# Both FFN products of a decoder layer by one level of Strassen's algorithm

## The chip, the cores and the metric

The kernel runs on one core of a Trainium2 chip. A core has TensorE (PE, with its weight loads as PEld), VectorE (DVE), ScalarE (ACT), GpSimd (POOL) and SyncE (SP, which here only issues transfers). The metric is device time in microseconds of one execution, the median of several runs.

## The reference, cut to what matters

One inference step of a one-layer decoder: 1024 prompt tokens and 8 x 4 sample tokens, together T = 1056 columns of width 1024. The token mixer (two attention branches, gates, output projection) stands first; the change lies behind its gates.

```python
def conv_ffn(h, conv_prev, w_up, conv_w, conv_b, w_down):
    t = h.shape[1]
    a, g = jnp.split(jnp.einsum('ntd,df->ntf', h, w_up), 2, axis=-1)
    ap = jnp.concatenate([conv_prev.astype(a.dtype), a], axis=1)
    c = conv_b
    for j in range(CONV_W):
        c = c + conv_w[j] * ap[:, j:j + t]
    y = jnp.einsum('ntf,fd->ntd', jax.nn.gelu(c, approximate=True) * g, w_down)
    return y, ap[:, t:]
...
    mixed = jax.nn.sigmoid(ga) * y_a + jax.nn.sigmoid(gb) * y_b
    return jnp.einsum('ntd,de->nte', mixed, w_out), new
...
    x = x + rmsnorm(mix, g_mix_post)
    f, new_conv = conv_ffn(rmsnorm(x, g_ffn_pre), conv_prev, w_up, conv_w, conv_b, w_down)
    x = x + rmsnorm(f, g_ffn_post)
```

D_MODEL is 1024, D_FF 4096, CONV_W 3; everything is in float32.

## The kernel before

Activations lie with features on the 128 partitions and tokens along the columns. Each float32 operand of a large product is *cut* in two parts, h and l, of a reduced format (fp32r in the rows), and a product takes three matmuls, wh x xh, wl x xh and wh x xl (`product`, L218; the matmul is L229). A weight unit of 128 x 1024 is loaded by SP into a `raw` tile (two of them), copied by ACT to wh (L94) and subtracted by POOL to wl (L95); the class `Stream` does this a few units ahead.

The tokens go through the output projection in three chunks of CH = 352 columns. For each chunk and each of 8 row tiles there are 24 matmuls; ACT squares the result and writes it to `mixed`. `post` (L1109) is a generator with the two norms that follow (after the mixer, before the FFN) of the chunk before; `advance` moves it on by steps between the products, by a table of numbers. A norm's statistics go through `spread` (L138): matmuls `ss` with ones add the squares over partitions, ACT and DVE make the factor 1/sqrt (`rstd_of`), DVE puts it on diagonals `dg`, and matmuls `rb` spread it to all partitions, in PSUM. The result, h2h and h2l, stays in SBUF for all tokens.

The FFN has 32 feature tiles f. For each, the up product makes a and g (two parts of three chunks, 24 matmuls each); behind part a, DVE runs the three-tap convolution over 1072 columns (L1214 to L1216) and ACT gelu (L1217); behind part g, DVE multiplies to u, ACT and DVE cut u to uh and ul (L1221, L1222). The down product of f (`down`, L1196: 24 groups of three matmuls of 352 columns, each added by DVE into `acc`, L1206) is put in portions of four groups behind the following up products. The last NL = 3 feature tiles' down products come in a last stage by 288, 256, 256 and 256 tokens, with the last norm (`final`, L1305) of each stretch beside the next one's matmuls.

The order on each engine is that in which the code emits instructions; each engine works through its own in order. All loads and stores of weights and activations here are issued by SP.

## Time and profile before

| what | value |
|---|---|
| time, median of 3 runs | 1975.89 us (1975.85 to 1976.13) |
| span of the profiled execution | 1977.6 us |
| PE busy | 1946.5 us (98%), 12418 instructions |
| DVE, ACT, POOL busy | 1015.3, 596.0, 527.1 us |
| output projection (732.60 to 862.80) | PE busy 127.47 of 130.20 us |
| FFN (862.80 to 1912.00) | PE busy 1049.20 of 1049.20 us |
| last stage (1912.00 to 1962.00) | PE busy 47.09 of 50.00 us |
| the FFN's traffic | 55 GB/s on a mean |

The profiled execution's span is 1.7 us longer than the median time. Busy time is the time in which an engine has an instruction under way; matmuls overlap, so their pace is read from the distance of their starts. Where a row of a timeline ends in a bracket, it says how long the engine stood idle before it and what ended that. The granted clock is a share of TensorE's full speed.

### The profile page before, as it was taken

Reading aid. Unit: us, or ns where it says so; the run is one execution under the profiler, and the core shown is the slowest. Engines: PE = TensorE matmul, PEld = TensorE weight load, DVE = VectorE, ACT = ScalarE, POOL = GpSimd, SP = SyncE. Lnnn points to the kernel's source line nnn. Section 1 sums busy time; section 2 is a strip of 40 time slices with the busy share of each in tenths; the row PEclk is TensorE's granted clock in tenths of the full one; section 3 lists DMA queues with packets and bytes.
Section 4 is the critical chain, followed back from the end, with each engine's and each line's share of the span. In section 5 each row is a group of like instructions: output and inputs, shape, how many; then the busy total and the mean of one; then the engine's idle time right before and its main releaser. Section 6 shows DMA issues by size and latency. Waiting matters only on the chain.

```text
span 1977.6 us, 30477 instructions
## 1 busy us (share of the span) xinstructions
PE 1946.5 (98%) x12418; PEld 1872.5 (95%) x12418; DVE 1015.3 (51%) x2221; ACT 596.0 (30%) x1365; POOL 527.1 (27%) x437
## 2 busy tenths in 40 slices
PE   7999999999999999999999999999999999999996
PEld 7977888888999999999999999999999999999996
DVE  7354437878611144774544545554455555445446
ACT  4365654444221134452211121121112112111233
POOL 3200025344333313422222222122222212222224
PEclk8999999999999999999999999999999999999998
DMA  5222145443422244711211121111111111111132
GB/s 204 71 73 75 69 116 168 137 131 122 162 80 94 84 153 180 289 54 65 75 65 54 64 85 50 58 54 43 54 44 43 53 34 54 44 54 44 43 116 88
DMA packets 63532, 175.15 MB, mean 89 GB/s; under 512 B 12720, under 2 KB 31216, under 8 KB 62192
## 3 DMA queue, kind: packets, MB, share of 16 engines
q1 hardware_dynamic: 61728, 172.72, 25.5%
q8 instruction: 97, 1.59, 0.3%
q10 hardware_dynamic: 1664, 0.49, 0.1%
q14 instruction: 43, 0.35, 0.1%
HBM read 160.21 MB, written 57.84 MB: 110 GB/s over the span
## 4 chain that ended last, share of the span: by engine, by line
PE 91%; DVE 5%; issue 1%; ACT 1%; POOL 0%; DMA 0%; SPq 0%; POOLq 0%; DVEq 0%; ACTq 0%
PE dense L229 84%; PE S L411 2%; PE O L483 2%; PE PT L471 2%; DVE sq L202 1%; DVE mixed L1319 1%; PE ss L144 0%; DVE mixed L1320 0%; DVE P L422 0%; PE rb L153 0%; DVE part L630 0%; DVE P L458 0%; DMA x<-in_x 0%; DVE d L434 0%; PE O L488 0%
## 5 line engine op out<-in xcount | busy, mean ns | idle before, releaser
L95 POOL TENSOR_TENSOR wl<-raw,wh 128x1024 fp32r<-128x1024 f32 (+1 forms) x110 | 261.1, 2373 | 996.6 <-ACT wh L94 787.2
L229 PE MATMUL dense<-h2h,wh 128*128 128x352 f32 x1536 | 495.7, 323 | 0.0
L229 PE MATMUL dense<-h2l,wh 128*128 128x352 f32 x1536 | 494.4, 322 | 0.0
L229 PE MATMUL dense<-h2h,wl 128*128 128x352 f32 x1536 | 493.0, 321 | 0.0
L1206 DVE TENSOR_TENSOR mixed<-dense,mixed 128x352 f32<-128x352 f32 x672 | 321.2, 520 | 147.5 <-PE dense L229 147.5
L229 PE MATMUL dense<-hh,wh 128*128 128x352 f32 x960 | 319.9, 336 | 2.4 <-ACT wh L94 1.9
L229 PE MATMUL dense<-hh,wl 128*128 128x352 f32 x960 | 307.5, 324 | 1.5 <-DVE wl L95 1.5
L229 PE MATMUL dense<-hl,wh 128*128 128x352 f32 x960 | 308.2, 325 | 0.0
L229 PEld LDWEIGHTS dense<-h2h,wl 128*128 128x128 f32 x1536 | 289.3, 188 | 0.0
L229 PEld LDWEIGHTS dense<-h2l,wh 128*128 128x128 f32 x1536 | 288.6, 188 | 0.0
L229 PEld LDWEIGHTS dense<-h2h,wh 128*128 128x128 f32 x1536 | 288.2, 188 | 0.0
L229 PE MATMUL dense<-uh,wdh 128*128 128x352 f32 (+2 forms) x792 | 254.8, 322 | 0.0
L229 PE MATMUL dense<-uh,wdl 128*128 128x352 f32 (+2 forms) x792 | 254.1, 321 | 0.0
L229 PE MATMUL dense<-ul,wdh 128*128 128x352 f32 (+2 forms) x792 | 254.0, 321 | 0.0
L229 PEld LDWEIGHTS dense<-hh,wh 128*128 128x128 f32 x960 | 180.9, 189 | 23.1 <-issue 14.0
L229 PEld LDWEIGHTS dense<-hh,wl 128*128 128x128 f32 x960 | 182.0, 190 | 1.9 <-DVE wl L95 1.9
L229 PEld LDWEIGHTS dense<-hl,wh 128*128 128x128 f32 x960 | 182.4, 191 | 0.0
L1239 ACT COPY a<-dense 128x352 f32<-128x352 f32 (+1 forms) x96 | 42.7, 445 | 372.3 <-PE dense L229 372.2
L1255 DVE TENSOR_TENSOR u<-dense,cv 128x352 f32<-128x352 f32 (+1 forms) x96 | 49.1, 511 | 206.1 <-PE dense L229 204.8
L229 PEld LDWEIGHTS dense<-uh,wdl 128*128 128x128 f32 x792 | 151.0, 191 | 0.0
L229 PEld LDWEIGHTS dense<-ul,wdh 128*128 128x128 f32 x792 | 150.8, 190 | 0.0
L229 PEld LDWEIGHTS dense<-uh,wdh 128*128 128x128 f32 x792 | 150.7, 190 | 0.0
(254 smaller groups left out, 2476.9 us busy)
## 6 DMA issues: line engine op xcount, KB each, us to landing
raw<-in_w_up SPq DMA_DIRECT2D x64, 512.0 KB, 3.4
out_s<-in_cache SPq DMA_DIRECT2D x32, 1022.0 KB, 8.0
raw<-in_w_in SPq DMA_DIRECT2D x40, 512.0 KB, 3.6
kv<-in_kv_s SPq DMA_DIRECT2D x64, 256.0 KB, 4.0
raw<-in_w_down SPq DMA_DIRECT2D x32, 512.0 KB, 3.5
out_s<-in_cache SPq DMA_DIRECT2D x8, 1016.0 KB
x<-in_x SPq DMA_DIRECT2D x12, 528.0 KB, 6.4
x2d<-mixed SPq DMA_DIRECT2D x3, 1408.0 KB
```

What stands on the lines that cost most here:

```text
L95: (eng or pool).tensor_tensor(l, raw, as32(h), op=OP.subtract)
L202: eng.tensor_tensor(o, o, x, op=OP.add)
L229: pe.matmul(ps, lhsT=w, rhs=x, start=(i == 0), stop=(i == len(mm) - 1))
L411: pe.matmul(S[h][:, 0:nk], lhsT=q[r, i * 128:(i + 1) * 128], rhs=k[r, blocks[i][0] * 128:blocks[i][0] * 128 + nk], start=True, stop=True)
L471: pe.transpose(PT[:, o:o + 128], s["P"][:, h, j * 128:(j + 1) * 128], ident)
L483: pe.matmul(O[64 * h:64 * h + 64, 0:128], lhsT=vt[:, kb * 128 + 64 * h:kb * 128 + 64 * h + 64], rhs=s["PTs"][:, (h * m + j) * 128:(h * m + ...
L1206: dve.tensor_tensor(acc[:, ct, cs], ps, acc[:, ct, cs], op=OP.add)
L1239: act.copy(at[:, 2 + c * CH:2 + c * CH + n], ps[:, :n])
L1255: dve.tensor_tensor(us_[:, c * CH:c * CH + n], ps[:, :n], cv[:, c * CH:c * CH + n], op=OP.mult)
L1319: (pool if own else dve).tensor_tensor(m, m, rs if own else rb, op=OP.mult)
```

## The change

Strassen's algorithm splits both operands of a product in 2 x 2 blocks and makes the four result blocks from seven products of sums of blocks instead of eight products of blocks; the form used here (Winograd's) has four sums of each operand.

*Output projection.* It runs in NQ = 4 quarters of CQ = 264 tokens instead of three chunks. `post` norms a quarter; for quarters 2 and 3 DVE also makes the token sums T1 to T4 out of the quarters' blocks, and `second_ops` cuts these operands. `advance` moves `post` by other numbers: ss and rb of a norm come in one step.

*Up product.* A unit m is one part (a or g) of a pair of feature tiles. For each of its seven products p, `up` issues two groups of 12 matmuls of 264 columns. POOL makes four sums of weight blocks for each m, and `cut_block` cuts a block of 128 x 512 (ACT copies, POOL subtracts) LA = 4 products ahead. `evac` takes results out of PSUM with DVE adds (ACT copies for p = 0). The convolution of a pair's second tile comes behind product 5 of part a, that of the first behind product 6, gelu behind each; u is made behind products of part g.

*u through DRAM.* `u_sums` makes four sums of u's blocks on DVE, and SP stores seven operands for each pair; the down product loads them back.

*Down product.* It comes after the whole up product: seven products, one at a time, each summed over all 16 pairs in all eight PSUM banks (four row tiles by two column groups; the last product in two halves of tokens). A step is 24 matmuls of 264 columns (12 in the halves) and needs a block of weights and an operand of u, loaded LOAD = 5 and cut CUT = 3 steps ahead; the weight sums are DVE's. `down_evac` adds a product's banks into acc. The last norm's parts (`squares_of`, `final`) are moved on by two steps behind each down step.

Besides, there are four `raw` tiles instead of two, tiles of the attention's phase have another side of the memory, and tables of the convolution have tiles of their own.

```diff
+CQ = 264
+NQ = 4
...
-        raw = wpool.tile([128, n], F32, name="raw", tag="raw", bufs=2, padded_shape=[128, 1024])
+        raw = wpool.tile([128, n], F32, name="raw", tag="raw", bufs=4, padded_shape=[128, 1024])
...
+    def cut_mixed(q, g, eng, new):
...
+        src = mixed[:, 4 * g:4 * g + 4, q * CQ:(q + 1) * CQ]
+        act.copy(h, src)
+        eng.tensor_tensor(l, src, as32(h), op=OP.subtract)
...
+    def op_cut(name, j, src, c=None):
...
+        dve.tensor_tensor(l, src, as32(h), op=OP.subtract)
...
+    def post(q, sums):
...
+        last = q == NQ - 1
+        g = spread(sums, CQ)
         next(g)
         yield
         rb = next(g)
...
         for ct in range(KT):
             m = mixed[:, ct, cs]
             dve.tensor_tensor(m, m, rb, op=OP.mult)
...
+            (dve if last or ct in (1, 3, 5) else pool).tensor_tensor(m, m, x3[q][ct // 4][:, ct % 4], op=OP.add)
+            sq.append(quarter("sq"))
+            act.activation(sq[-1], m, AF.Square)
+            if len(sq) > 2:
+                total(sums, sq.pop(0), pool if last else dve)
             if ct == KT - 1:
...
+        g = spread(sums, CQ)
         next(g)
         yield
         rb = next(g)
...
+        for k in range(KT):
+            o = x3[q][k // 4][:, k % 4] if last else mixed[:, k, cs]
+            dve.scalar_tensor_tensor(o, mixed[:, k, cs], gains[:, 2, k:k + 1], rb, op0=OP.mult, op1=OP.mult)
+            if k % 2:
...
+        t2 = x3[2][c]
+        for j in range(2):
+            b1, b2 = rows(2 * j, q), rows(4 + 2 * j, q)
+            b11, b21 = rows(2 * j, q - 2), rows(4 + 2 * j, q - 2)
+            dve.tensor_tensor(b11, b1, b11, op=OP.subtract)
+            dve.tensor_tensor(t2[:, 2 * j:2 * j + 2], b2, b11, op=OP.subtract)
+            dve.tensor_tensor(b1, b2, b1, op=OP.subtract)
+            dve.tensor_tensor(b21, b21, t2[:, 2 * j:2 * j + 2], op=OP.subtract)
+            yield
...
+    def second_ops():
...
+        for name in ("T2", "T3", "T4", "B22", "T1"):
...
+                    q = 2 + c
+                    src = {"T2": x3[2][c][:, 2 * j:2 * j + 2], "T3": rows(2 * j, q), "T4": rows(4 + 2 * j, c),
+                           "B22": rows(4 + 2 * j, q), "T1": rows(2 * j, c)}[name]
+                    op_cut(name, j, src, c)
+                yield
...
+    PRODUCTS = (("A11", "B11"), ("A12", "B21"), ("S2", "T2"), ("S3", "T3"), ("A22", "T4"), ("S1", "T1"), ("S4", "B22"))
...
+    def cut_block(src):
+        t = wpool.tile([128, 2, 512], F32R, name="whl", tag="W", bufs=6)
+        act.copy(t[:, 0], src)
+        pool.tensor_tensor(t[:, 1], src, as32(t[:, 0]), op=OP.subtract)
+        return t
...
+    def up_cut(m, p):
...
+        r1, r2 = uraw[m, 0], uraw[m, 1]
+        a11, a12, a21, a22 = r1[:, 0:512], r1[:, 512:], r2[:, 0:512], r2[:, 512:]
+        if p == 2:
+            s = usum[m] = T_("S", n=1024), T_("S", n=1024)
+            pool.tensor_tensor(s[0][:, 0:512], a21, a22, op=OP.add)
+            pool.tensor_tensor(s[0][:, 512:], s[0][:, 0:512], a11, op=OP.subtract)
+        elif p == 3:
+            pool.tensor_tensor(usum[m][1][:, 0:512], a11, a21, op=OP.subtract)
+        elif p == 6:
+            pool.tensor_tensor(usum[m][1][:, 512:], a12, usum[m][0][:, 512:], op=OP.subtract)
+        if p in (0, 1, 4):
+            src = (a11, a12, None, None, a22)[p]
+        else:
+            s = usum[m]
+            src = {2: s[0][:, 512:], 3: s[1][:, 0:512], 5: s[0][:, 0:512], 6: s[1][:, 512:]}[p]
+        uhl[m, p] = cut_block(src)
...
+    def conv(f):
...
+        dve.tensor_scalar(o, at[:, 0:SEQ], w[0], w[3], op0=OP.mult, op1=OP.add)
+        dve.tensor_scalar(so, fr[:, :, 0:4], w[0], w[3], op0=OP.mult, op1=OP.add)
+        for x in (1, 2):
+            dve.scalar_tensor_tensor(o, at[:, x:x + SEQ], w[x], o, op0=OP.mult, op1=OP.add)
+            dve.scalar_tensor_tensor(so, fr[:, :, x:x + 4], w[x], so, op0=OP.mult, op1=OP.add)
+        act.activation(cv, cv, AF.Gelu_apprx_tanh)
+        pool.tensor_copy(ncv[:, f, 0:2], at[:, SEQ:SEQ + 2])
+        pool.tensor_copy(ncv[:, f, 2:18].rearrange("p (b s) -> p b s", s=2), fr[:, :, 4:6])
...
+    def evac(m, p, c, ps):
...
+        if p == 0:
+            act.copy(s[:, cs], ps)
+            return
...
+        if p == 3:
+            dve.tensor_tensor(t[:, cs], ps, s[:, cs], op=OP.add)
+            return
+        if p == 5:
+            dve.tensor_tensor(s[:, cs], ps, s[:, cs], op=OP.add)
+        fo = f + (p in (4, 5))
+        base = t if p in (4, 5) else s
+        q = c + 2 * (p in (5, 6))
+        if part == 0:
+            put_a(fo, q, lambda o, z: dve.tensor_tensor(o, seen(z, ps), seen(z, base[:, cs]), op=OP.add))
+            return
...
+        o = fpool.tile([128, CQ], F32, name="tm", tag="tm", bufs=2) if p in (1, 4) else base[:, cs]
+        dve.tensor_tensor(o, ps, base[:, cs], op=OP.add)
+        cv = fs[fo][2]
+        qs = slice(q * CQ, (q + 1) * CQ)
+        dve.tensor_tensor(cv[:, qs], o, cv[:, qs], op=OP.mult)
...
+    def up(m, p, mid=None):
...
+            for k in range(4):
+                ks = slice(128 * k, 128 * k + 128)
+                wh, wl, xh, xl = w[:, 0, ks], w[:, 1, ks], op_at(bname, 0, k, c), op_at(bname, 1, k, c)
+                mm += [(wh, xh), (wl, xh), (wh, xl)]
+            for i, (l, r) in enumerate(mm):
+                pe.matmul(ps, lhsT=l, rhs=r, start=(i == 0), stop=(i == len(mm) - 1))
+            evac(m, p, c, ps)
...
+        if part == 0 and p in (5, 6):
+            f = 2 * fp + (p == 5)
+            fs[f].append(fpool.tile([128, T], F32, name="cv", tag="cv", bufs=3))
+            conv(f)
+        if part == 1 and p == 6:
+            u_sums(fp)
...
+    def u_sums(fp):
...
+        dve.tensor_tensor(ta[:, 0], uf[:, h2], uf[:, h1], op=OP.subtract)
+        dve.tensor_tensor(ta[:, 1], ug[:, h2], uf[:, h2], op=OP.subtract)
+        dve.tensor_tensor(tb[:, 0], ug[:, h2], ta[:, 0], op=OP.subtract)
+        dve.tensor_tensor(tb[:, 1], ug[:, h1], tb[:, 0], op=OP.subtract)
+        def store():
+            sp.dma_start(d[:, 0], uf[:, h1])
+            sp.dma_start(d[:, 1:3].rearrange("p i t -> p (i t)"), ug)
+            sp.dma_start(d[:, 3:5], ta)
+            sp.dma_start(d[:, 5:7], tb)
...
+    FP = FT // 2
+    DOWN = (("A11", "B11"), ("S3", "T3"), ("S1", "T1"), ("S2", "T2"), ("S4", "B22"), ("A22", "T4"), ("A12", "B21"))
+    dseq = [(p, fp, None) for p in range(6) for fp in range(FP)] + [(6, fp, c) for c in range(2) for fp in range(FP)]
...
+    def down_load(i):
...
+        p, fp, c = dseq[i]
+        f = 2 * fp
+        if p == 0:
+            resident[fp] = X_("wr", F32)
+            sp.dma_start(resident[fp][:, 0:512], a["w_down"][f][:, 0:512])
+        elif p == 1:
+            sp.dma_start(resident[fp][:, 512:1024], a["w_down"][f][:, 512:])
+        elif p in (2, 4, 5) or (p == 6 and c == 0):
+            r = draw[p, fp] = wpool.tile([128, 512], F32, name="raw", tag="raw", bufs=4, padded_shape=[128, 1024])
+            sp.dma_start(r, a["w_down"][f + 1][:, 512:] if p in (2, 5) else a["w_down"][f + 1][:, 0:512])
+        n = CQ if c is not None else 2 * CQ
+        t = dxr[i] = T_("ur", n=n)
+        b = UD[DOWN[p][1]]
+        sp.dma_start(t, ud[fp][:, b, (c or 0) * CQ:(c or 0) * CQ + n])
...
+    def down_cut(i):
...
+                r = resident[fp]
+                a11, a21 = r[:, 0:512], r[:, 512:1024]
+                if p == 1:
+                    src = T_("S3", n=512)
+                    dve.tensor_tensor(src, a11, a21, op=OP.subtract)
+                elif p == 2:
...
+            if p == 6 and fp < 4:
+                kept[fp] = cut_block(src)
...
+            else:
+                dw[i] = cut_block(src)
+        x = dxr[i]
+        n = x.shape[1]
+        t = dx[i] = T_("uc", F32R, 2 * n).rearrange("p (x n) -> p x n", x=2)
+        act.copy(t[:, 0], x)
+        dve.tensor_tensor(t[:, 1], x, as32(t[:, 0]), op=OP.subtract)
...
+    LOAD, CUT = 5, 3
...
+    def down(i):
...
+        for j in range(4):
+            ks = slice(128 * j, 128 * j + 128)
+            for cc in range(2) if c is None else (c,):
...
+                ps = dbanks[j, cc]
+                xs_ = slice(cc * CQ, (cc + 1) * CQ) if c is None else slice(0, CQ)
+                for n, (l, r) in enumerate(((w[:, 0, ks], x[:, 0, xs_]), (w[:, 1, ks], x[:, 0, xs_]), (w[:, 0, ks], x[:, 1, xs_]))):
+                    pe.matmul(ps, lhsT=l, rhs=r, start=(fp == 0 and n == 0), stop=(fp == FP - 1 and n == 2))
...
+    def down_evac(p, c):
...
+            elif p == 3:
+                t = tm[j, cc] = quarter("u2")
+                dve.tensor_tensor(t, ps, c11, op=OP.add)
+            else:
+                o = {4: c12, 5: c21, 6: c11}[p]
+                dve.tensor_tensor(o, ps, o, op=OP.add)
+        if p == 3:
+            for j, cc in js:
...
+                dve.tensor_tensor(c21, c21, t, op=OP.add)
+                dve.tensor_tensor(c22, c21, c12, op=OP.add)
+                dve.tensor_tensor(c12, c12, t, op=OP.add)
...
+    early0, early = (0, 1), {}
+    QUEUE = [(0, 0), (0, 1), (1, 0), (1, 1)] + [(m, p) for m in range(2) for p in range(2, 7)]
+    QUEUE += [(m, p) for m in range(2, FT) for p in range(7)]
+    for q in range(NQ):
...
+        if q < NQ - 1:
+            for g in range(2):
+                cut_mixed(q + 1, g, dve, X_)
         for ct in range(KT):
...
+            advance((2, 3, 3, 3, 3, 3, 3, 9)[ct])
+            if ct == 5 and q:
+                load_rows(q)
+            if q == NQ - 1 and ct in (3, 4, 5, 6):
+                up_cut(*QUEUE[ct - 3])
...
+        step = post(q, sums)
...
+    step = chain(step, second_ops())
+    LA = 4
...
+    for i, (m, p) in enumerate(QUEUE):
+        if i == 4:
+            advance(40)
...
+        if i + LA < len(QUEUE):
+            up_cut(*QUEUE[i + LA])
+        else:
+            down_cut(i + LA - len(QUEUE))
+        up(m, p, lambda: advance({0: 1, 1: 4, 2: 4, 3: 4}.get(i, 0)))
+        if p == 2 and m > 0:
+            up_load(m + 1, 0)
+            up_load(m + 1, 1)
+        if p == 3 and stores:
+            stores.popleft()()
...
+        if m == FT - 1 and p > 0:
+            down_load(p - 1)
...
+    for i in range(len(dseq)):
+        p, fp, c = dseq[i]
+        down_load(i + LOAD)
+        down_cut(i + CUT)
+        down(i)
+        if fp == FP - 1:
+            down_evac(p, c)
+            if p == 4:
+                load_x4(1, X_)
+                step = chain(squares_of(2, range(KT), fsums[2]), squares_of(3, range(KT), fsums[3]))
+            elif p == 5:
+                step = chain(step, squares_of(0, range(4, 8), fsums[0]), squares_of(1, range(4, 8), fsums[1]), final(2, fsums[2]),
+                             final(3, fsums[3]))
+            elif (p, c) == (6, 0):
+                load_x4(0, T_)
+                step = chain(step, squares_of(0, range(4), fsums[0]), final(0, fsums[0]))
+            elif (p, c) == (6, 1):
+                step = chain(step, squares_of(1, range(4), fsums[1]), final(1, fsums[1]))
+        advance(2)
+    advance(100)
```

Where instructions stand. First PE in the output projection: before, behind a product of the second chunk, the ss matmuls of a norm (L144), and the rb matmuls (L153) that need DVE's answer to them; `mh`, `ml`, `woh`, `wol` are the two parts of the mixer's output and of its weights.

```order
L229 MATMUL dense<-ml,woh 128x352
L144 MATMUL ss<-ones,sq 128x1 x6
L229 MATMUL dense<-mh,woh 128x352
L229 MATMUL dense<-mh,wol 128x352
L229 MATMUL dense<-ml,woh 128x352
...
L229 MATMUL dense<-ml,woh 128x352
L153 MATMUL rb<-dg,ones 128x128 x2
L153 MATMUL rb<-dg,ones 128x96
```

Between ss and rb stand 24 matmuls, a whole product. In the changed kernel the same place, in a quarter, reads:

```order
L232 MATMUL dense<-mh,wol 128x264
L232 MATMUL dense<-ml,woh 128x264
L147 MATMUL ss<-ones,sq 128x1 x6
L156 MATMUL rb<-dg,ones 128x128 x2
L156 MATMUL rb<-dg,ones 128x8
L232 MATMUL dense<-mh,woh 128x264
```

No product is left between the two.

Second, ACT in the FFN. Before: `wh` and `wdh` are copies of weights of the up and the down product, `uh` the copy of u, `a` the results for the convolution, `cv` gelu.

```order
L94 CAST wh<-raw 128x1024
L1221 CAST uh<-u 128x1056
L1239 COPY a<-dense 128x352
L94 CAST wh<-raw 128x1024
L1239 COPY a<-dense 128x352
L94 CAST wdh<-raw 128x1024
L1239 COPY a<-dense 128x320
L1242 COPY a<-dense 128x8x4
L1217 ACTIVATE cv<-cv 128x1072
L94 CAST wh<-raw 128x1024
```

There is one gelu for a feature tile, behind the copies of a. In the changed kernel, for a pair (`whl` is a cut block, `S` a sum of weight blocks, `u_...` product 0):

```order
L1240 CAST whl<-S 128x512
L1287 ACTIVATE cv<-cv 128x1056
L1240 CAST whl<-S 128x512
L1287 ACTIVATE cv<-cv 128x1056
L1240 CAST whl<-raw 128x512
L1316 COPY u_11852<-dense 128x264 x2
L1240 CAST whl<-S 128x512 x2
L1240 CAST whl<-raw 128x512 x2
```

The two gelus stand close together, and the copies of the blocks for products 3 and 4 of part g stand behind the first and the second of them.

## Rows read from the trace of the kernel before

**Rows 1.** The page: busy time of each engine, and the chain by line.
```profile
PE 1946.5 (98%) x12418; PEld 1872.5 (95%) x12418; DVE 1015.3 (51%) x2221; ACT 596.0 (30%) x1365; POOL 527.1 (27%) x437
...
PE dense L229 84%; PE S L411 2%; PE O L483 2%; PE PT L471 2%; DVE sq L202 1%; DVE mixed L1319 1%; PE ss L144 0%; DVE mixed L1320 0%; DVE P L422 0%; PE rb L153 0%; DVE part L630 0%; DVE P L458 0%; DMA x<-in_x 0%; DVE d L434 0%; PE O L488 0%
```
**Rows 2.** Windows: stretch, us, busy PE PEld DVE ACT POOL (count), clock, DMA, GB/s.
```profile
0.00:50.00 50.00, 39.23 (x198) 35.96 (x199) 38.48 (x60) 21.52 (x33) 16.58 (x11) 0.90 0.59 205
732.60:862.80 130.20, 127.47 (x813) 127.16 (x812) 82.02 (x159) 59.33 (x117) 46.95 (x41) 0.99 0.56 206
862.80:1912.00 1049.20, 1049.20 (x6553) 1049.20 (x6552) 525.51 (x947) 212.28 (x316) 237.54 (x216) 1.00 0.16 55
1912.00:1962.00 50.00, 47.09 (x346) 46.34 (x344) 32.55 (x89) 25.80 (x63) 23.30 (x30) 0.90 0.27 100
```
**Rows 3.** Timeline of PE: start, duration, engine, line; ends of two even runs.
```profile
1839.73 0.32 PE L229 MATMUL dense<-h2l,wh 128*128 128x352 f32 x1
...
1858.26 0.32 PE L229 MATMUL dense<-h2h,wl 128*128 128x352 f32 x1
...
1930.18 0.28 PE L229 MATMUL dense<-uh,wdl 128*128 128x256 f32 x1
...
1936.37 0.28 PE L229 MATMUL dense<-ul,wdh 128*128 128x256 f32 x1
```
**Rows 4.** Timeline, all engines: from ss to the three dg of one norm.
```profile
802.56 0.36 PE L144 MATMUL ss<-ones,h 128*128 128x1 f32 x2
...
802.96 0.26 ACT L128 ACTIVATE s<-ss,eps 128x3 f32<-128x3 f32 x1 [0.26 <-PE ss L144]
...
804.19 0.68 DVE L148 TENSOR_SCALAR dg<-ident,r 128x128 f32<-128x128 f32 x3
```
**Rows 5.** A wait of PE in the timeline, the clock behind it (window), the chain there.
```profile
830.15 1.41 PE L153 MATMUL rb<-dg,ones 128*128 128x128 f32 x6 [2.73 <-DVE dg L148]
...
832.00:834.00 2.00, 2.00 (x9) 2.00 (x9) 1.94 (x5) 0.97 (x2) 2.00 (x2) 0.56 1.01 366
...
831.55 6.87 PE dense L229 x36
```
**Rows 6.** Groups by shape: busy us, mean ns of one; idle time before, its releasers.
```profile
L95 POOL TENSOR_TENSOR wl<-raw,wh 128x1024 fp32r<-128x1024 f32 x102 | 246.3, 2415 | 959.7 <-ACT wh L94 750.3 <-DVE mixed L1206 195.0 <-PE dense L229 5.9
L607 POOL TENSOR_TENSOR kv<-kv,qs 128x512 f32<-128x512 f32 x32 | 40.6, 1294 | 25.4 <-DMA kv<-in_kv_s 14.6 <-DVE d L434 5.0 <-DVE e L452 3.6
L1339 DVE TENSOR_TENSOR mixed<-dense,mixed 128x256 f32<-128x256 f32 x24 | 9.6, 413 | 4.6 <-PE dense L229 4.6
L1215 DVE SCALAR_TENSOR_TENSOR cv<-a,cws,cv 128x1072 f32<-128x1072 f32 x30 | 40.0, 1334 | 1.1
L1214 DVE TENSOR_SCALAR cv<-a,cws 128x1072 f32<-128x1072 f32 x30 | 25.4, 847 | 121.1 <-ACT a L1242 121.1
L1222 DVE TENSOR_TENSOR ul<-u,uh 128x1056 fp32r<-128x1056 f32 x30 | 37.8, 1258 | 35.8 <-ACT uh L1221 35.8
L94 ACT CAST wh<-raw 128x1024 fp32r<-128x1024 f32 x107 | 111.6, 1043 | 32.6 <-PE dense L229 9.3 <-issue 7.4 <-DMA raw<-in_w_out 6.8
L1217 ACT ACTIVATE cv<-cv 128x1072 f32<-128x1072 f32 x30 | 33.1, 1102 | 113.9 <-DVE cv L1216 113.9
```
**Rows 7.** Timeline of POOL and DVE: two POOL operations and what DVE did.
```profile
803.73 0.16 DVE L132 SCALAR_TENSOR_TENSOR t<-t,r 128x3 f32<-128x3 f32 x1
...
826.41 2.37 POOL L95 TENSOR_TENSOR wdl<-raw,wdh 128x1024 fp32r<-128x1024 f32 x1
826.52 2.28 DVE L132 SCALAR_TENSOR_TENSOR t<-t,r 128x3 f32<-128x3 f32 x1
...
1231.22 1.92 DVE L1206 TENSOR_TENSOR mixed<-dense,mixed 128x352 f32<-128x352 f32 x4
1231.36 2.40 POOL L95 TENSOR_TENSOR wl<-raw,wh 128x1024 fp32r<-128x1024 f32 x1 [5.60 <-ACT wh L94]
```
**Rows 8.** DMA issues: queue, count, KB each, median us from issue to landing.
```profile
raw<-in_w_up SPq DMA_DIRECT2D x64, 512.0 KB, 3.4
```

More of the change, by code (lines that the diff above doesn't have):

```diff
@@ L1115, in post @@
         rb = next(g)
-        q, sums = [], []
+        sq, sums = [], []
         for ct in range(KT):
@@ L1309, in final @@
+    def final(q, sums):
+        cs = slice(q * CQ, (q + 1) * CQ)
+        hs = slice(q % 2 * CQ, (q % 2 + 1) * CQ)
+        last = q == 1
+        g = spread(sums, CQ)
         next(g)
```

454 lines of the change are left out of this document (237 added, 217 removed).

## The prediction

> **What bounds the kernel now.** I read the page's busy shares and its chain first, then the busy time by stage, then TensorE's pace, then groups of instructions by shape. PE is busy 98% of the span, and 84% of the chain is one line, the dense matmuls [rows 1]. By stage: in the FFN (862.80 to 1912.00) PE and its weight loads are busy all of the 1049.20 us at full granted clock, with DVE at half and ACT and POOL under a quarter; in the output projection it lacks 2.7 us of 130.2, at the very end 2.9 of 50, at the start 10.8 of 50 [rows 2]. So only fewer matmul columns can make this kernel much faster, and what is taken away is counted at TensorE's pace. That pace follows the columns: 116 matmuls of 352 columns took 18.53 us, 0.1597 each; 52 of 256 took 6.19 us, 0.1190 [rows 3] (the durations in the rows overlap; the starts give the pace). By a line through the two, 264 columns take 0.1224 and 288 take 0.1326.
>
> **The change part by part**, against the profiled span of 1977.6 us, which is 1.7 above the median of 1975.89.
>
> 1. *FFN matmuls.* Before: 6696 of 352 columns (4608 up, 2088 down), 72 of 288, 216 of 256: 1069.4 + 9.5 + 25.7 = 1104.6. After: 32 x 7 x 24 up and 96 x 24 + 32 x 12 down, 8064 of 264 columns at 0.1224 = 987.0. **-118**, all on the path. The column count falls by an eighth; narrower matmuls give back some 14 us of it.
>
> 2. *Output projection in quarters.* 768 matmuls at 0.1224 are 94.0 against 576 at 0.1597, 92.0; a fourth quarter has its own two spreads (6 ss at 0.18 each, 3 rb) of some 1.5 us (by 0.18 an ss [rows 4]). **+5**.
>
> 3. *Its waits.* Before, the ss matmuls go to PE one product ahead of the rb matmuls that need their answer. After, rb stands right behind ss, so PE waits through ACT's square root and DVE's Newton step: from ss at 802.56 to the end of the first dg at 804.87 are 2.3 us [rows 4]. It does so twice for each of quarters 1 to 3: 2.3 + 2.0. The second ss also waits for the eight tiles' multiply, add and sum (some 1.0 us each on DVE by the 0.41 row [rows 6]) which three products, 8.8 us, don't quite cover: 1.8. Before, one rb waited 2.73 us; the granted clock then read 0.56, mostly the lower of its two levels (1.2 and 2.4 GHz), and the next 36 matmuls took 6.87 us where 36 x 0.1597 is 5.75: 1.1 lost [rows 5]. With two such drops a quarter costs 6.1 + 2.2 = 8.3; three are 24.9, less before's 3.8: **+21** (8 if the waits stay too short for the clock and half hidden, 30 if POOL's adds trail).
>
> 4. *Handover to the up product.* The four products issued first need only quarters 0 and 1: 11.7 us of cover. The third product of the first pair needs T2, hence the whole norm of the last quarter: two spreads (4.3), eight tiles (8.0) and their last sums (1.9), eight scalings of 0.41, eight differences of 0.63 and the cut (0.55 + 0.63) twice [rows 6]: 24.9. That leaves 13 us of waiting, with 2.2 for two clock drops and some 3 for the later operands, which follow one another through the same DVE and ACT: **+18** (10 to 28).
>
> 5. *Up product, 16 pairs of feature tiles.* PE needs 14 x 2.94 = 41.1 us for a pair. The convolution of the pair is now whole, and runs at two products of part a; behind it on ACT's in-order queue stand gelu and, behind gelu, the copies for later weight cuts. Product 4 of the g part is cut only after the second gelu. From the end of product 5 of part a: evacuation 1.0 (two adds of 0.41), convolution 0.85 + 2 x 1.33 + three small pieces = 3.8, evacuation 1.2 (with the sample tokens' piece), convolution 3.8, gelu 1.1, copy 0.55 (half the 1024 row), POOL's subtract 1.29, hand-offs 0.6: 13.3 [rows 6]. The cut is due five products later, 14.7: a slack of 1.4. But POOL now makes 22 tiles of 512 columns for a pair (14 cuts, 8 sums), 22 x 1.29 = 28.5 us, and DVE operations with two operands in SBUF stand still beside a POOL operation: at 826.41 POOL subtracted for 2.37 us, and a three-column operation that takes 0.16 took 2.28 beside it [rows 7]. A DVE operation that reads PSUM kept its pace (four in 1.92 us) [rows 7]. If POOL still works off cuts when the convolutions begin, two or three of the six long operations wait for a subtract of 1.3: 2.6 to 3.9, of which the slack hides 1.4. That is 1.2 to 2.5, and some half of a clock drop, 0.6, as such a stall is about as long as that in rows 5. I take 2.5 us a pair, in 15 pairs: **+37**. The ends: nothing, if the lead covers it; 84, in rival B. For the rest, by the same rows DVE has some 25 us of work for a pair and ACT 12 of gelus, copies and cuts, both under 41.
>
> 6. *Down product.* Seven products, each held in all 8 banks; PE could run through, but at three places it can't. After product 3, 8 + 24 DVE adds of 0.41 are 13 us where three steps of lead are 8.8: +4. In the first half of product 6 a step has 12 matmuls, 1.47 us, while POOL subtracts for each step 1.29 and also takes 16 adds of about 0.65 for the sums of squares and final norms: 16 x 1.29 + 10 = 31 against 23.5: +8. The x tiles for the last norm, 2.1 MB, stand ahead of u loads on SP's queue: +3. The final norms are spread over matmuls as before. **+15** (5 to 35).
>
> 7. *Start and end.* Four raw tiles instead of two let weight loads go out earlier, in a stretch where PE lacks 10.8 us [rows 2]: -3 (-6 to +1); the tail is longer by a few 264-wide pieces: +1. **-2**.
>
> Sum: -118 + 5 + 21 + 18 + 37 + 15 - 2 = -24: a span of 1953.6, hence a time of **1952**.
>
> **The rivals.**
>
> A. *The lead covers the locks.* Four products ahead and a slack of 1.4 us suffice; the up product runs at PE's pace: term 5 is 0, the time 1952 - 37 = 1915. For it: POOL has 28.5 of 41.1 us to do, and before it idled most of the FFN (237.54 us of 1049.20 [rows 2]). Against it: the second gelu's chain alone takes 13.3 of 14.7 us.
>
> B. *The pair is set by POOL and DVE, which stand in each other's way: slower than before.* POOL's 28.5 and DVE's two-operand work (convolutions 7.6, eight products of u at 0.41, four sums at 0.63, small pieces 0.4: 13.8) come one after the other, with the two gelu-and-copy waits of 1.65 in which POOL has nothing: 45.6 us for a pair of 41.1. PE waits 4.5 in one stretch, long enough for the clock, +1.1: 5.6 x 15 = 84 for term 5, so 1952 + 47 = 1999. It decides from a wait of 4.1 us a pair, where 24 us more than in term 5 are gone. For it: the 2.28 us in rows 7. Against it: POOL's work can slide into PSUM evacuations, which aren't held. The Trainium skill has a rule for this ("SBUF — State Buffer", Who interferes with whom): a DVE instruction with two SBUF inputs and a GpSimd instruction that reads SBUF contend for a shared port pair, as an exclusive lock for the whole instruction, and it calls DVE instructions with at most one SBUF input outside the perf modes free of it. By that rule the sum of both engines' times is the floor of this rival; the trace agrees with it in both pairs of rows 7.
>
> C. *The down product is bound by its loads.* Each of its steps brings 256 KB of weights and 264 KB of u, where u was in SBUF before. One load of 512 KB took 3.4 us from issue to landing [rows 8]: 520 KB would be 3.45 for 2.94 us of matmuls, over 80 full steps +41, and 388 KB for 1.47 us over the 16 half steps, +18: 1952 + 59 = 2011. Against it: five steps of loads are in flight, and 366 GB/s were moved at 832 to 834 [rows 5], twice what is needed.
>
> That the change doesn't do what it says is no case here: the order of the changed kernel has the 8064 matmuls of 264 columns.
>
> **How the numbers follow.** A run tells 0.2%, about 4 us, from no change. The forecast (a wait of 1 to 3.6 us a pair, 1930 to 1969) gets 0.44; A 0.22; B 0.22, a quarter of it within 0.2% of 1976; C 0.10; 0.02 is left, halved between faster and same. Faster: 0.44 + 0.22 + 0.01 = 0.67; same: 0.05 + 0.01 = 0.06; slower: 0.17 + 0.10 = 0.27. The range leaves out half a tenth of A at its low end, where terms 3, 4 and 6 are at their lower bounds too, C, and B's upper quarter: **1900 to 2005**. The forecast's own range is 1930 to 1969.
>
> **What would show it.** TensorE's pace of 0.122 us a matmul shows term 1; were it nearer 0.14, the gain is half. Waits of rb on DVE's dg of 2 us, six in the output projection, with clocks under 1 behind them, show term 3. In the FFN I look for PE waiting once for each pair, at product 3 or 4 of a g part, for POOL's whl, and for convolutions longer than 1.33: near 0 says A, 5 says B. PE waiting for a cut of u that waits for a DMA in the down product says C. Wrong in another way would be a wait in each product, or a clock that stays low.

## The result, and the profile after

The changed kernel takes 1995.21 us (median of 4 runs, 1988.62 to 1998.16) against 1976.01 for the kernel before (1975.85 to 1978.79, 4 runs): a ratio of 1.0089, interval 1.007 to 1.0108. It is slower, where 1952 and faster were forecast. The time lies at rival B's 1999, but B's mechanism isn't what happened: the up product hardly waits.

The page of the changed kernel: span, busy time, granted clock in 40 slices, and the chain by engine.

```profile
span 1992.5 us, 35225 instructions
...
PE 1877.2 (94%) x13708; PEld 1793.6 (90%) x13708; DVE 1233.5 (62%) x2437; ACT 701.5 (35%) x1648; POOL 999.4 (50%) x822
...
PEclk8999999999999998887999999999999999998988
...
POOL 25%; PE 8%; issue 8%; ACT 5%; DVE 4%; DMA 2%; SPq 0%; ACTq 0%; POOLq 0%; DVEq 0%
```

Against [rows 1] PE's busy time fell by 69 us only, and PE now lacks 115 us of the span instead of 31. The clock is under 0.9 in the 16th to 19th slice, the output projection and what follows it, and at the end of the down product. As windows (us, busy PE, PEld, DVE, ACT, POOL with counts, clock, DMA share, GB/s) a stretch of the output projection, the first pair of feature tiles, the other fifteen pairs, and the down product to its last matmul:

```profile
780.00:830.00 50.00, 37.27 (x253) 36.86 (x253) 26.57 (x69) 15.74 (x39) 11.24 (x14) 0.80 0.56 196
...
877.90:958.30 80.40, 57.46 (x368) 55.52 (x367) 65.63 (x118) 26.92 (x51) 40.51 (x38) 0.79 0.20 70
958.30:1582.10 623.80, 617.59 (x5042) 614.34 (x5041) 489.71 (x804) 170.30 (x306) 526.26 (x450) 1.00 0.30 99
1582.10:1976.20 394.10, 355.40 (x2726) 350.95 (x2724) 238.98 (x333) 156.42 (x307) 177.57 (x146) 0.94 0.50 160
```

The first line is a stretch of the output projection: 37 of 50 us busy at a clock of 0.80, where [rows 2] showed 127.47 of 130.20 at 0.99 (of a stretch whose last 26 us are up product already). The second is the first pair, 80.4 us for what takes 41.6 later; DVE is the busiest engine in it. The third, fifteen pairs, is dense at full clock. The fourth, the down product, is not.

What PE waited for in the output projection and the first pair (725 to 960), and in the down product (1575 to 1992): us in total, times, longest.

```profile
PE ss L147 <- DVE sq L1116: 17.8, 4, 6.4
PE rb L156 <- DVE dg L151: 15.4, 7, 4.4
PE dense L1366 <- DVE T L1144: 9.0, 4, 4.2
...
PE rb L156 <- DVE dg L151: 11.5, 4, 5.8
PE dense L1477 <- DVE acc L1491: 11.2, 2, 6.5
PE ss L147 <- POOL sq L1116: 4.6, 2, 3.0
PE dense L1477 <- DVE u L1494: 4.3, 1, 4.3
```

The waits that were forecast for ss and rb are there. The one nobody forecast is `acc L1491`, 6.5 and 4.7 us: PE waits for banks to be emptied between products of the down product, where the emptying itself takes DVE 1.44 us for its four copies.

By stages, in us of the two profiled executions, with the working of the prediction's terms beside what was measured (a stage's end is the start of the next one's first matmul):

| stage | before | after | forecast | measured |
|---|---|---|---|---|
| up to the output projection | 732.7 | 738.7 | -3 | +6.0 |
| output projection | 103.6 | 139.2 | +26 | +35.6 |
| FFN to its last matmul | 1125.6 | 1098.3 | -48 | -27.3 |
| tail | 15.7 | 16.3 | +1 | +0.6 |
| span | 1977.6 | 1992.5 | -24 | +14.9 |

### The profile page after: what moved, and what is told of

It reads as the page before. It is cut to its first block, busy times and chain, and to the rows that moved or that the text cites. A ratio compares the mean times of both kernels' runs of the same rounds, so it can differ in the third digit from the quotient of the medians.

```text
span 1992.5 us, 35225 instructions
## 1 busy us (share of the span) xinstructions
PE 1877.2 (94%) x13708; PEld 1793.6 (90%) x13708; DVE 1233.5 (62%) x2437; ACT 701.5 (35%) x1648; POOL 999.4 (50%) x822
## 4 chain that ended last, share of the span: by engine, by line
POOL 25%; PE 8%; issue 8%; ACT 5%; DVE 4%; DMA 2%; SPq 0%; ACTq 0%; POOLq 0%; DVEq 0%
POOL whl L1241 15%; PE dense L1477 6%; ACT whl L1240 3%; POOL S L1263 2%; POOL S L1265 2%; POOL S L1260 2%; POOL S L1261 2%; PE dense L1366 2%; POOL ncv L1289 2%; ACT uc L1459 1%; DMA wr<-in_w_down 1%; DMA ur<-ud 1%; DVE uc L1460 1%; DVE raw L1446 0%; DMA raw<-in_w_down 0%
## 5 line engine op out<-in xcount | busy, mean ns | idle before, releaser
L1366 PE MATMUL dense<-T,whl 128*128 128x264 f32 x3072 | 390.3, 287 | 18.3 <-DVE T L1144 9.0
L1366 PEld LDWEIGHTS dense<-T,whl 128*128 128x128 f32 x3072 | 382.6, 191 | 22.9 <-POOL whl L1241 11.0
L1477 PE MATMUL dense<-uc,whl 128*128 128x264 f32 x2400 | 310.7, 293 | 25.7 <-DVE acc L1491 11.2
L1477 PEld LDWEIGHTS dense<-uc,whl 128*128 128x128 f32 x2400 | 306.8, 196 | 29.2 <-ACT acc L1489 11.6
L1241 POOL TENSOR_TENSOR whl<-S,whl 128x512 fp32r<-128x512 f32 x144 | 233.0, 1618 | 128.0 <-ACT whl L1240 128.0
L98 POOL TENSOR_TENSOR wl<-raw,wh 128x1024 fp32r<-128x1024 f32 (+1 forms) x46 | 106.5, 2315 | 377.5 <-ACT wh L97 367.6
L1366 PE MATMUL dense<-B,whl 128*128 128x264 f32 x2304 | 290.6, 286 | 0.0
L1366 PEld LDWEIGHTS dense<-B,whl 128*128 128x128 f32 x2304 | 286.6, 190 | 0.0
L1460 DVE TENSOR_TENSOR uc<-ur,uc 128x528 fp32r<-128x528 f32 (+1 forms) x128 | 147.9, 1159 | 136.5 <-ACT uc L1459 134.2
L1241 POOL TENSOR_TENSOR whl<-raw,whl 128x512 fp32r<-128x512 f32 x132 | 178.9, 1367 | 93.4 <-ACT whl L1240 93.4
```

The costliest lines, as they stand in the source:

```text
L98: (eng or pool).tensor_tensor(l, raw, as32(h), op=OP.subtract)
L1241: pool.tensor_tensor(t[:, 1], src, as32(t[:, 0]), op=OP.subtract)
L1366: pe.matmul(ps, lhsT=l, rhs=r, start=(i == 0), stop=(i == len(mm) - 1))
L1460: dve.tensor_tensor(t[:, 1], x, as32(t[:, 0]), op=OP.subtract)
L1477: pe.matmul(ps, lhsT=l, rhs=r, start=(fp == 0 and n == 0), stop=(fp == FP - 1 and n == 2))
```

## The experiments

Each edit stands against the changed kernel, if nothing else is said. Where no rounds are named, a kernel ran once beside the kernel before, which took 1976.1 to 1977.9 in these comparisons.

**A product between ss and rb.**

```diff
-            advance((2, 3, 3, 3, 3, 3, 3, 9)[ct])
+            advance((1, 4, 4, 0, 1, 4, 2, 9)[ct])
```

> The changed kernel with one line edited: in the output projection the steps of the norms are dealt out as 1, 4, 4, 0, 1, 4, 2, 9 instead of 2, 3, 3, 3, 3, 3, 3, 9, so that a whole product (24 matmuls) stands between each ss and its rb, and between the eighth tile and the second ss. Theory: the 45 us that the stage takes beyond its matmuls (139.2 us from 738.7 to 877.9 against 94) are PE's waits for the norm's chain (six for dg, 11.0 us, three for sq, 11.4 us) and the lower clock behind each; they go, the stage falls to some 105 us, and the time from 1995 to about 1962. Rival: the chain of a quarter (some 20 us on DVE) is longer than its cover wherever the matmuls stand; the waits only move to other products, the stage stays above 125 us and the time above 1980.

Measured: 1969.0. The output projection takes 112.8 us (736.7 to 849.5) instead of 139.2. The same stretch as above, as a window (us, busy PE, PEld, DVE, ACT, POOL with counts, clock, DMA share, GB/s):

```profile
780.00:830.00 50.00, 49.69 (x412) 49.48 (x411) 34.17 (x84) 22.47 (x55) 14.97 (x20) 1.00 0.69 251
```

PE is busy throughout, the clock is 1.00, and 412 matmuls were recorded in the place of 253. The waits were the order's, not the chain's: 26 us by moving a few instructions of PE past 24 others. It stays 7 us over the 105 expected: one rb wait of 4.7 us is left, and the 105 had little for the ss and rb matmuls themselves.

**u copied ahead of the weights in the down product.** The feed of a step of the down product, in the changed kernel's timeline (start, duration, idle before it and what ended that), where the weights are a sum:

```profile
1684.65 1.41 DVE L1460 TENSOR_TENSOR uc<-ur,uc 128x528 fp32r<-128x528 f32 x1 [1.27 <-ACT uc L1459]
1685.98 0.68 DVE L1440 TENSOR_TENSOR wr<-wr,raw 128x512 f32<-128x512 f32 x1
1687.93 1.41 DVE L1460 TENSOR_TENSOR uc<-ur,uc 128x528 fp32r<-128x528 f32 x1 [1.27 <-ACT uc L1459]
1689.26 1.44 DVE L1491 COPY acc<-dense 128x264 f32<-128x264 f32 x4
...
1686.75 0.62 ACT L1240 CAST whl<-wr 128x512 fp32r<-128x512 f32 x1 [2.13 <-DVE wr L1440]
1687.28 0.63 ACT L1459 CAST uc<-ur 128x528 fp32r<-128x528 f32 x1
...
1687.51 1.27 POOL L1241 TENSOR_TENSOR whl<-wr,whl 128x512 fp32r<-128x512 f32 x1 [2.01 <-ACT whl L1240]
...
1689.83 2.54 PE L1477 MATMUL dense<-uc,whl 128*128 128x264 f32 x10 [6.51 <-DVE acc L1491]
```

Read it in a ring. DVE makes a sum of weights (1685.98); ACT, which has waited 2.13 us for it, copies it and then u (1686.75, 1687.28); DVE, which has waited 1.27 us for u's copy, subtracts, in 1.41 as POOL's subtract runs beside it (1687.51), where the same operation takes 0.70 by itself (1683.98 in the rows of the next run); only then comes DVE's next sum. No engine is busy for even two thirds of it, and all wait: 3.28 us from one `uc` to the next, against 2.92 us of matmuls (24 at the 0.1218 measured below, a little more than the 2.87 expected). Sixteen steps fall behind by 5.7 us. PE doesn't see it step by step: it lives on three steps of lead until the product's end, where the evacuation (1689.26) stands behind the late cuts on DVE's queue, and PE, out of banks, waits 6.51 us.

```diff
     def down_cut(i):
...
+        act.copy(t[:, 0], x)
         if c != 1:
...
-        act.copy(t[:, 0], x)
         dve.tensor_tensor(t[:, 1], x, as32(t[:, 0]), op=OP.subtract)
```

> The changed kernel with one order edited: in the cut of a step of the down product, ACT copies the operand of u ahead of the block of weights instead of behind it. Theory: the down product's feed is a ring of one step, DVE's sum of weights 0.68, ACT's two copies 1.06, DVE's subtract of u 1.4 beside POOL's, with hand-offs 3.3 us, against 2.87 us of matmuls; where a product has a sum (four of seven) the lead is used up and the evacuation comes 4 to 6.5 us late. With u copied first the ring is open (DVE 2.1 us a step): the waits of 6.5, 4.7 and 2.6 us at the ends of products go, with the lower clock behind them, and the time falls from 1995 by 15 to 25, to 1970 to 1980. Rival: the waits are those for eight banks to be emptied, or for loads of u and weights; then they stay and the time stays within 5 us of 1995.

Measured: 1969.4. The down product takes 367 us instead of 394. PE's timeline over the stretch in which it waited 6.51 us, and DVE's:

```profile
1635.82 64.38 PE L1477 MATMUL dense<-uc,whl 128*128 128x264 f32 x527
...
1683.38 0.68 DVE L1444 TENSOR_TENSOR wr<-wr,raw 128x512 f32<-128x512 f32 x1
1683.98 0.70 DVE L1460 TENSOR_TENSOR uc<-ur,uc 128x528 fp32r<-128x528 f32 x1
1684.60 0.68 DVE L1444 TENSOR_TENSOR wr<-wr,raw 128x512 f32<-128x512 f32 x1
```

PE runs over the end of a product (1682.83) without a break, and DVE's sum and subtract follow one another without waiting. The same loads, copies, sums and locks are all there; one copy changed its place in ACT's queue. So neither the loads (rival C) nor the banks by themselves set those waits.

**Three products ahead instead of four in the up product.** `LA = 4` becomes `LA = 3`.

> The changed kernel with the up product's weights cut three products ahead instead of four. Theory: the chain from the end of product 5 of part a over both convolutions, the second gelu and the cut of the block for product 4 of part g takes 15.2 us in the trace, 0.5 over the 14.7 us that five products cover; with three ahead it is due for the block of product 3 or 4 with one product (2.94 us) less cover: PE waits about 3.4 instead of 0.5 us a pair, with a lower clock behind it, 15 pairs give +40 to +60 and a time of 2035 to 2055. Rival: POOL works 85% of this stage and sets the pace by its sum, not by a chain; then the lead matters little and the time stays within 10 us of 1995.

Measured: 2030.4. The up product takes 746.7 us (875.5 to 1622.2) instead of 704.2. PE's waits from 960 to 1610, then PE around one such wait:

```profile
PE dense L1366 <- POOL whl L1241: 35.4, 23, 2.0
...
1204.34 3.05 PE L1366 MATMUL dense<-T,whl 128*128 128x264 f32 x23 [1.83 <-POOL whl L1241]
1207.55 0.39 PE L1366 MATMUL dense<-T,whl 128*128 128x264 f32 x1 [0.16 <-ACT whl L1240]
1208.90 8.90 PE L1366 MATMUL dense<-T,whl 128*128 128x264 f32 x71 [0.96 <-POOL whl L1241]
```

A pair takes 44.6 us instead of 41.6, which is one product less of cover, and the waits stand at products 2 and 3 of part g (counted from 0). The chain of the prediction's term 5 is right, and with four products ahead it is covered to within half a microsecond. The time came out 5 us under the range, since the other stages took 7 us less in that run and the first pair 3.

**The first pair without the last quarter's operands.**

```diff
         aname, bname = PRODUCTS[p]
+        if m < 2 and p > 1:
+            bname = "B11"
```

> The changed kernel, but products 2 to 6 of the first pair of feature tiles read operand B11 instead of T2, T3, T4, T1 and B22 (so their results are others); no work is left out. Theory: from the first up product at 877.9 to the end of the first pair at 958.3 are 80.5 us for 41.1 us of matmuls, since five products need operands from the last quarter's norm, a chain of DVE and ACT longer than its cover of four products, and the clock falls in the waits. Without that dependence the dense matmuls of the pair wait for nothing but weights; the ss and rb matmuls of the last quarter still stand in PE's order and wait. The pair takes 55 to 62 us and the time falls by 18 to 25, to 1970 to 1977. Rival: cutting the weights (POOL and ACT start late) or evacuation sets this stretch; then it stays above 72 us and the time within 8 us of 1995.

Measured: 1995.6; the up product takes 703 us, against 704, and its first pair 79.3, against 80.4. The theory falls. PE's waits between 870 and 965, and in DVE's timeline what stood ahead of the evacuation:

```profile
PE dense L1368 <- DVE u L1322: 6.3, 1, 6.3
...
PE dense L1368 <- DVE early L1337: 3.4, 1, 3.4
...
913.02 4.76 DVE L1144 TENSOR_TENSOR T<-x,T 128x528 fp32r<-128x528 f32 x4
...
928.69 3.62 DVE L1144 TENSOR_TENSOR T<-mixed,T 128x528 fp32r<-128x528 f32 x4
932.23 0.76 DVE L1322 TENSOR_TENSOR u<-dense,u 128x264 f32<-128x264 f32 x2
```

PE no longer waits for operands and waits for banks instead: product 2 is evacuated at 932.23, behind the 20 subtracts of `op_cut` on DVE's queue. That points to DVE's own queue, in the changed kernel busy for 65.63 us of the 80.4, but doesn't show it: the last quarter's ss and rb, which stand between the products on PE, wait 5.9 and 4.0 us here too, and the clock is as low.

**The tiles' place, in the kernel before.** The change's side edits were tried on the kernel before, since the same 352-column matmuls of the first 700 us started every 0.1623 us in the changed kernel and every 0.1600 before. First four raw tiles and the smaller reserve (`bufs=4`, `dynamic_dma_scratch_size=1024`):

> The kernel before with four raw weight tiles instead of two and the smaller reserve for transfer descriptors that makes room for them (two of the change's side edits). Question: in the changed kernel the same 352-column matmuls of the first 700 us start every 0.1623 us instead of 0.1600, which costs 6 us by the output projection. If these two edits do it, by where tiles come to lie or by transfers beside them, the pace here is 0.162 and the time 1976 + 15 or so; if not it stays 0.160 and the time within 3 us of 1976.

Measured: 1979.0, pace 0.1603. Not these. Then the pool of the normed input at the other end of the memory, alone:

```diff
-    cpool = ctx.enter_context(tc.tile_pool(name="cpool", bufs=1))
+    cpool = ctx.enter_context(tc.tile_pool(name="cpool", bufs=1, side="right"))
```

> The kernel before with one side edit of the change alone: the tiles of the normed input (hh, hl, mh, ml) and their pool stand at the other end of the memory. The four raw tiles and the smaller reserve left the pace of the 352-column matmuls at 0.1603 us. If the place of these tiles is what slows the same matmuls in the changed kernel, the pace here is 0.162 and the output projection begins some 6 us later than at 732.7; if not, it stays 0.160 and the cause is left with the width of the other tiles (1056 instead of 1074 columns), which can't be changed in this kernel by itself.

Measured: 1993.8, pace 0.1620. PE's 12418 instructions stand in the order of the kernel before; the edit moves addresses alone. As a window of the FFN, to be read against [rows 2]:

```profile
862.80:1912.00 1049.20, 1049.20 (x6485) 1048.93 (x6484) 520.33 (x946) 211.28 (x314) 232.68 (x213) 1.00 0.16 53
```

PE is busy all of the time at full clock in both, and 6485 matmuls instead of 6553 fit in. Between 1300 and 1400 the matmuls that read h2h and h2l from these tiles start the next one 0.1640, 0.1603 and 0.1623 us later (wh, wl, and h2l), before 0.1602, 0.1591 and 0.1596; those of uh and ul, which lie elsewhere, 0.1609 in both. The tiles' addresses say why that may be: 161760 here, 32 over a multiple of 64 bytes; 52480 before, a multiple. So, 32 unused bytes at that end:

```diff
+    rpad = ctx.enter_context(tc.tile_pool(name="rpad", bufs=1, side="right"))
+    rpad.tile([128, 8], F32, name="rpad")
     cpool = ctx.enter_context(tc.tile_pool(name="cpool", bufs=1, side="right"))
```

> The kernel before with the normed input's tiles at the other end of the memory, as in the run that took 1993.8, and 32 unused bytes at that end. In that run all instructions and waits were as before, but matmuls whose moving operand lies in these tiles start 1.5% later each (0.1624 against 0.1597 us; those of uh and ul 0.1608 as before), and the tiles begin at an address of 32 over a multiple of 64 bytes (161760), where before they begin at a multiple (52480). The 32 bytes move them to 161728. If the remainder does it, the pace is back at 0.160 and the time at 1976 to 1979; if it is the end of the memory, it stays at 1990 or more.

Measured in three rounds: 1979.68 (1977.46 to 1982.12), ratio 1.0011, 1.0002 to 1.002. The window again:

```profile
862.80:1912.00 1049.20, 1049.20 (x6545) 1049.20 (x6545) 525.86 (x947) 212.21 (x317) 237.66 (x216) 1.00 0.16 54
```

32 bytes give back 14 of the 16 us, so the end of the memory by itself is not the cause. Neither is the remainder by itself. The tiles of uh and ul, in the kernel before, start at both remainders: where both lie 32 over a multiple, the 143 groups of three matmuls between 862 and 1912 come every 0.1606 us each, where both lie at a multiple, the 240 groups every 0.1613 (the addresses of the built kernel, joined with the trace in order). The slow pace was seen only with both, this end and this remainder; between the last two runs no tile moved but those of this pool.

**The same 32 bytes in the changed kernel, alone.**

> The changed kernel with nothing but the 32 unused bytes at the end of the memory. It says how much of the change's +19 us is the address of its tiles, apart from the two orders and the handover. By the step from 1933.7 to 1924.6 under the four edits: 9 us less than 1995.2, 1986 (1981 to 1991), so still slower than before by some 0.5%; of it 6 us stand ahead of the output projection (it begins at 733 instead of 738.7). If the address only matters where no other wait is behind it, 1990 or more.

Measured in three rounds: 1988.95 (1988.52 to 1989.94), ratio 1.0062, 1.0046 to 1.0079. The output projection begins at 731.4 instead of 738.7; the stages behind it keep their lengths (140.9, 703.5 and 394.8 us). So the address cost some 6 us of the 19 (6.3 by the medians, 7.3 at the start of the output projection; one of the changed kernel's four runs took 1988.62 too), and the changed kernel is slower without it too.

**Together.** Both orders, and then two more edits in the down product (DVE's 24 adds behind product 3 dealt out two at a time; four steps of the generator instead of one between ss and rb of the last norm):

> The changed kernel with both edits that helped: a product between ss and rb in the output projection, and u copied ahead of the weights in the down product. They act in different stages, one took 26 us off and the other 26: if the gains add, 1943 (1938 to 1948), 0.983 of the kernel before; if both freed the same slack behind a third thing, 1960 or more.

> As the one with both edits, and two more in the down product: DVE's 24 adds behind product 3 are dealt out two at a time over the next six steps instead of at once, and in the last norm two steps stand between ss and rb. Theory: the burst of 10.3 us after product 3 and the rb waits of 5.8 and 2.7 us in the last product, each with a lower clock behind it, go: 10 to 14 us less, 1930 (1926 to 1936). Rival: in the last product the loads, which stand behind the stores of y on SP's queue, are late by themselves; then the rb waits turn into waits for whl or uc and at most 6 us are won.

Measured in three rounds each: 1941.65 (1939.41 to 1942.72), ratio 0.9817, 0.9802 to 0.9832: the gains add. With the two further edits 1933.68 (1928.6 to 1934.23), ratio 0.9779, 0.9763 to 0.9795; the down product falls from 367.5 to 356.4 us. Then the 32 bytes, and the operands' cuts behind the first evacuation:

> As the kernel with four edits (1933.7), and the same 32 bytes at that end of the memory, where the changed kernel has the normed input, and later the up product's operands B and T. If the remainder of the address sets the pace: the 352-column matmuls of the first 738 us go from 0.1624 to 0.160 (-6 us), and half of the up product's, whose second column group lies 1056 bytes on, change with it in either direction (no net gain): 1927 (1922 to 1931). If it is the end of the memory, 1933 as before.

> As the one with 32 bytes, and the cuts of the operands T3, T4, T1 and B22 issued behind product 2 of the first unit instead of ahead of it. Theory: the run without the operands' dependence showed that the handover is not a wait for operands but DVE's queue: 20 cuts of 0.7 to 1.8 us stand ahead of the first evacuations there, and PE runs out of banks. With 16 of them behind, product 2 is evacuated in time: 4 to 8 us less than the kernel with 32 bytes alone. Rival: the cuts are needed by the next products anyway, so the wait moves from banks to operands, within 2 us.

Measured: 1924.6 (1924.28 to 1925.19), ratio 0.9736, 0.9719 to 0.9752 (9 us by the medians; the profiled executions differ by 4.3, all of it ahead of the output projection); and 1921.81 (1919.78 to 1923.99), ratio 0.9721, 0.9706 to 0.9735. The last step is worth 2.8 us where 4 to 8 or under 2 were expected, and settles little: PE's waits between 840 and 940 in that kernel are still these.

```profile
PE ss L149 <- DVE sq L1118: 6.8, 1, 6.8
PE dense L1368 <- DVE T L1146: 6.6, 2, 4.5
PE rb L158 <- DVE dg L153: 5.1, 1, 5.1
```

The handover's cost is left in all versions. The last of them beats the kernel before by 2.8%, 56 us, and the changed one by 73.

## Why the prediction was wrong, step by step

The sign was wrong, and the failed step is term 6: "PE could run through, but at three places it can't". There were more places than three, and the largest was not among them. The term's miss, 31 us, is by itself more than the 24 us that were forecast to be won; term 4 is next, short by 21.

1. *FFN matmuls*, -118: right. In the up product 96 matmuls start in 11.68 us, 0.1217 each, by these two rows:

```profile
1213.66 11.84 PE L1366 MATMUL dense<-T,whl 128*128 128x264 f32 x96
1225.34 8.94 PE L1366 MATMUL dense<-B,whl 128*128 128x264 f32 x72
```

   In the down product it is 0.1218, as in the 527 of the row of 64.38 us above. 5376 and 2688 of them are 982 us instead of 987: -123. The straight line between two widths was 0.5% off. (By the prediction's own numbers narrower matmuls give back 20 us of the eighth, not 14; its sum doesn't use that.)
2. and 3. *Output projection and its waits*, +26: mechanism right, size short; +35.6. The rb waits are 1.7 to 2.4 as worked out (though 804.87 is the end of all three dg, not of the first); the second ss waits 3.8 us a quarter instead of 1.8, as these rows of a quarter show:

```profile
821.45 1.44 PE L147 MATMUL ss<-ones,sq 128*128 128x1 f32 x6 [3.79 <-DVE sq L1116]
824.66 1.42 PE L156 MATMUL rb<-dg,ones 128*128 128x128 f32 x6 [1.76 <-DVE dg L151]
```

   That the waits go with the order was shown by the first experiment, 26 us. More is lost to the clock. The windows of the dense matmuls alone (us, busy PE with count, clock, DMA share, GB/s), for the output projection, the first pair and the down product:

```profile
738.70:877.90 139.20, 102.75 (x770) 0.88 0.54 193
877.90:958.30 80.40, 52.54 (x338) 0.79 0.20 70
1582.10:1976.20 394.10, 349.67 (x2690) 0.94 0.50 160
```

   At the pace of the full clock they would be busy 93.5, 40.9 and 327.4. By this estimate the lower clock behind the waits costs 9, 12 and 22 us, where terms 3, 4 and 6 had 6.6, 2.2 and nothing for it.
4. *Handover*, +18: 39.5 us (80.4 against 40.9). I worked out the latency of one chain to the first operand, 13 us of waiting, and 3 for the later operands. PE waits 22.9: 9.0 for operands, 6.4 and 4.4 for the last quarter's own ss and rb, which stand between the products in its order, and 3 for weights; with them goes the clock, 12 us instead of 2.2. What sets the waits stays open: without the operands' dependence those for operands became waits for banks, with 16 of the 20 cuts issued later they were for operands again, and the stretch got shorter by 1 and by 3 us only.
5. *Up product*, +37: 10 us, and rival A's mechanism. The chain is where it was said to be. In the timeline of one pair of the changed kernel, DVE, ACT, POOL and PE:

```profile
1226.37 1.60 DVE L1282 TENSOR_SCALAR cv<-a,cw 128x1024 f32<-128x1024 f32 x1
...
1228.10 1.27 DVE L1285 SCALAR_TENSOR_TENSOR cv<-a,cw,cv 128x1024 f32<-128x1024 f32 x1
1229.30 1.27 DVE L1286 SCALAR_TENSOR_TENSOR cv<-fr,cw,cv 128x32 f32<-128x32 f32 x1
1230.49 1.27 DVE L1285 SCALAR_TENSOR_TENSOR cv<-a,cw,cv 128x1024 f32<-128x1024 f32 x1
...
1237.63 1.09 ACT L1287 ACTIVATE cv<-cv 128x1056 f32<-128x1056 f32 x1 [3.89 <-DVE cv L1286]
1238.63 0.61 ACT L1240 CAST whl<-raw 128x512 fp32r<-128x512 f32 x1
...
1228.16 2.37 POOL L1241 TENSOR_TENSOR whl<-S,whl 128x512 fp32r<-128x512 f32 x1 [0.73 <-ACT whl L1240]
...
1239.31 1.29 POOL L1241 TENSOR_TENSOR whl<-raw,whl 128x512 fp32r<-128x512 f32 x1 [1.82 <-ACT whl L1240]
...
1240.66 6.00 PE L1366 MATMUL dense<-T,whl 128*128 128x264 f32 x47 [0.43 <-POOL whl L1241]
```

   From the end of product 5 at some 1225.5 to the cut block at 1240.6 are 15.1 us, for a cover of 14.7: PE waits 0.43. The locks took 3.1 us of the two convolutions (1.60 for an operation that takes 0.81 by itself, 1.27 for one of 32 columns that takes 0.24 elsewhere; in the second convolution 1.03 and 1.28 for the same two), within the 2.6 to 3.9 of the term. It is the chain without them that was too long, 13.3 instead of 12.0: I added durations that overlap by up to a tenth of a microsecond from one row to the next, and a slack of one microsecond was the whole term. And POOL stands still too, twice in this pair: its subtract took 2.37 instead of 1.29 while the long convolution (1228.10) kept its 1.27. The Trainium skill ("SBUF — State Buffer", Who interferes with whom) says that issue order, not the operation's shape, decides who blocks; the rows agree (the convolution started 0.06 us ahead of the subtract). Rival B summed both engines' times as if nothing else could run between them; the pair takes 41.6 us (20.44 + 21.15), not 45.6.
6. *Down product*, +15: 394.1 us for 327 of matmuls, 67 lost where 21 were lost in the FFN before, so +46. The ring of a step was not worked out at all, though its parts were known: DVE's sum, two copies on one queue, and from term 5 the lock, which makes a subtract of 0.70 into 1.4. I compared engines' sums with PE's time (in term 5 "both under 41", here POOL's alone) and never followed one step around; nor had the term anything for the clock. Opening the ring took 27 us off the stage; dealing out the adds and parting the last ss and rb, other mechanisms in this term, 11 more.
7. *Start and end*, -2: +6.6. That tiles change their place was taken as free. It cost some 6 us by the address; it was no rival, as no row of before could show it.

Together: -123 + 35.6 + 39.5 + 10.4 + 45.7 + 6.6 = +14.8, against the measured +14.9. Rival C isn't seen: ACT waits 18 us in all for loads of u in the changed kernel, but with the order changed the same loads kept up. The chain of the profiled execution names POOL first, with 25%; that is the way through the up product's cuts, which were just covered, and not where the time was to be gained.

## What to carry to other kernels

When a stage is handed a new supply chain, follow one step of it around all the queues it passes, with the order in which each engine has the step's instructions, and compare that round with the consumer's time: each engine's busy share says nothing of a ring, and a lead of a few steps hides it until the next place where everything has to be empty. In such a ring, and between a reduction and its use, look first for the one instruction whose place in an in-order queue closes it; here two such places were worth 26 us each, more than the whole difference to be explained. Count with each wait the lower clock behind it: in the three stages with waits PE stood idle for 84 us, and the clock cost some 43 more. And when only memory is laid out anew, compare the pace of the same matmuls before anything else.

## What the runs showed of the hardware that was not expected

The place of a matmul's moving operand can change its pace. With 352 columns of four bytes, at the far end of the memory and 32 over a multiple of 64 bytes, matmuls followed one another every 0.1622 us on a mean; moved by 32 bytes, every 0.1600; in the kernel before, every 0.1597. The granted clock was the same, and PE and its weight loads were busy throughout. Over the 4608 of the up product and the 2880 on hh ahead of it this made 16 us. It is no rule of the remainder alone: uh and ul at the same remainder, elsewhere in the memory, kept 0.1606. What it is, and which widths and remainders count, stays open; in the changed kernel's up product, with 264 columns, the 32 bytes changed nothing (0.1217 a matmul with and without them).
